# Hybrid decoder trunk on one core: the sums of squares behind the hand-overs move from VectorE to GpSimd

## The chip, the cores and the metric

The kernel runs on one core of one Trainium2 chip. The metric is device time in microseconds (us) of one execution, taken as the median over the runs of the kernel. TensorE, VectorE (DVE in the profile), ScalarE (ACT) and GpSimd (POOL) each work through a queue of instructions in order; the order of every queue is fixed when the kernel is built.

## What is computed

Two layers of a decoder trunk over 272 positions (16 meta tokens and 256 real ones) and 2048 channels, in float32. Cut to what matters here:

```python
def rms_norm(x, g):
    y = x * rsqrt(mean(x * x, axis=-1) + EPS)
    return y * g

def hybrid_layer(x, ...):
    h = rms_norm(x, norm_mix_pre)
    proj = h @ w_in                       # four groups of heads follow
    mix = concat([o_diff, o_sb, o_ssm, o_ret])
    x = x + rms_norm(mix @ w_out, norm_mix_post)
    hf = rms_norm(x, norm_ffn_pre)
    ffn = (silu(hf @ w_gate) * (hf @ w_up)) @ w_down
    return x + rms_norm(ffn, norm_ffn_post)
```

Each layer has four norms over 2048 channels. The two called "pre" stand behind a residual add and ahead of a large product.

## The kernel before

Activations lie with channels on the 128 partitions: `x` is 16 chunks (KC = 16) of 128 x 272. Weights stream from HBM in units of 8 tiles of 128 x 128 (`raw`, three buffers). Each unit is split into two parts: ScalarE copies the rounded high part (`hi`, line 682), VectorE subtracts it from the raw unit (`lo`, line 694), and TensorE makes three matmuls for each tile (`tile_mm`, line 711), high times high, high times low, low times high; in the second layer's feed-forward part two matmuls, the first of double width (`pair_mm`, line 733). Up to four units are held split (SPB = 4). The raw buffer of a unit is free for the next DMA when its `lo` is done (lines 696 to 698).

**The hand-overs.** When a product that ends in a residual add is finished, `norm` (line 1884) makes the post norm of chunk 0, and `post` (line 1956) goes through the other chunks in batches of one to three: VectorE scales `y`, adds it into `x`, ScalarE writes the high part of the next product's input `xhl` and VectorE its low part (`low`, line 1960). TensorE starts the next product at once, with the input not yet normalised: `first_chunk` (line 748) and `run_group` (line 773) go through the 16 chunks for 7 output tiles in 7 banks of PSUM. The pre norm's factor is a number for each position and is applied afterwards, when VectorE takes the products out of PSUM and multiplies by `rbc` (`evac_in`, line 1755; `evac_gu`, line 2020).

`prenorm` (line 1680) finds that factor beside the products. Behind the three hand-overs (layer 0 in its middle, layer 0 to layer 1, layer 1 in its middle) it calls `sumsq2` (line 1659): ScalarE squares two chunks at a time into one of two buffers (`squares`, line 1664), VectorE adds each square into `a2` (line 1675), seven times, and at the end adds the two halves of `a2` into `acc` (line 1678). TensorE then sums `acc` over the partitions in one matmul into `pn` (line 1685), and ScalarE and VectorE make `rbc` from it (`rsqrt_m2`, line 830). `prenorm` in the first layer's start has no `sq` and goes through `sumsq` (line 1642).

In the page the adds are `yf<-yf` (middle of a layer, where the squares lie in `yf`) and `sq<-sq` (between the layers). VectorE's instructions all carry line 338, those of ScalarE 378, matmuls 397: the helpers that record them.

**What sets the order.** While the kernel is built, a planner (`Sched`, line 461) advances threads against a model of the engines (`Clock`, line 238): each instruction has a modelled cost, each engine a modelled time, and a thread's next step is issued when its inputs are near ready in that model (`ok`, line 515). The matmul into `pn` goes into TensorE's queue where the model has `acc` ready. On the chip each queue is worked off in that order, whatever the real times are.

Of the kernel before, what the change touches and what calls it, by code (L numbers as in the profile page):

```python
# [16 lines left out]
ALU = mybir.AluOpType  # L17
# [220 lines left out]
class Clock:  # L238
# [1 line left out]

    LOG = None

    LAT = {"P": 0.2, "V": 0.14, "A": 0.145, "D": 0.0, "X": 0.0}

    def __init__(self):
        self.t = {"P": 0.0, "V": 0.0, "A": 0.0, "D": 0.0}
        self.acc = {}
        self.prev = {}
        self.slots = {}
        self.dead = set()  # L250
        self.step_end = 0.0
        self.win, self.cols, self.fast = 0, 0.0, False
# [19 lines left out]
    def ready(self, ap, eng, write=False):  # L272
        name, lo, hi = self.region(ap)
        r = 0.0
        for a in self.acc.get(name, ()):
            if a[0] < hi and lo < a[1]:
                r = max(r, a[2] + (self.same(eng) if a[3] == eng else self.LAT[a[3]]))
                if write:
                    r = max(r, a[4])
        return r  # L280
# [4 lines left out]
    def op(self, eng, cost, outs, ins, lat=0.0, cols=None):  # L285
# [28 lines left out]
        if eng != "D":  # L314
            self.step_end = max(self.step_end, en + self.LAT[eng])
        return en


def _free(ap):
    n = 1  # L320
    for d in ap.shape[1:]:
        n *= d
    return n


def _psum(ap):
    return "PSUM" in str(ap.space)


class Vec:  # L330
# [3 lines left out]
    def __getattr__(self, name):  # L334
        fn = getattr(self.eng, name)

        def f(*args, **kw):
            r = fn(*args, **kw)  # L338
            if args:
                kw = dict(kw, out=args[0])  # L340
            out = kw["out"]
            ins = [v for k, v in kw.items() if k in ("in_", "in0", "in1", "data0", "data1") and hasattr(v, "ap")]
            sc = [v for k, v in kw.items() if k in ("scalar", "scalar1", "scalar2") and hasattr(v, "ap")]
            n = max([_free(out)] + [_free(a) for a in ins])
            ps = any(_psum(a) for a in ins + [out])
            fast = name in ("tensor_scalar", "tensor_copy", "memset") and not ps
            cost = 0.068 + n / (1920.0 if fast else 960.0) + 0.061 * len(sc)
            if name == "reciprocal":
                cost = 0.07 + n * 0.0063
            self.clk.op("V", cost, [out], ins + sc)  # L350
            return r
        return f


class Act:
# [105 lines left out]
class Sched:  # L461
# [9 lines left out]
    def add(self, gen, prio, ready=0.0):  # L471
        th = Thread()
        th.gen, th.prio, th.done, th.end = gen, prio, False, ready
        th.ready = ready
        self.threads.append(th)
        self._advance(th)
        return th
# [86 lines left out]
def hybrid_trunk_kernel(ctx, tc, xT, wst, prm, ssm, b3, gpo, cst, msk, out, cfg=None, dbg=None):  # L564
    cfg = cfg or {}
    nc = tc.nc
    clk = Clock()
    V, A, PE = Vec(clk, nc.vector), Act(clk, nc.scalar), Ten(clk, nc.tensor)
    sched = Sched(clk, A, {"V": cfg.get("LV", 1.2), "A": cfg.get("LA", 1.0), "slack": cfg.get("slack", 0.15), "low": cfg.get("low", 0.4), "tab": cfg.get("tab", 4.0)})
    NU = wst.shape[0]  # L570
    RAWB = cfg.get("raw", 3)
    SPB = cfg.get("spl", 4)
# [46 lines left out]
    P = const.tile([128, DEPTH, NPC], F32, name="P")  # L619
# [931 lines left out]
    acc = rb_p.tile([128, T], F32, name="acc")  # L1551
# [107 lines left out]
    def sumsq2(src, n, sq, ready, prio):  # L1659

        qs = []
        a2 = sq(0)

        def squares():
            for k in range(0, KC, 2):
                yield ("A", lambda: ready(k + 1) if len(qs) < 2 else None)
                q = a2 if k == 0 else sq(1 + k // 2 % 2)
                A.activation(out=q, in_=src[:, k:k + 2], func=AF.Square)
                if k:
                    qs.append(q)  # L1670

        sched.add(squares(), prio)
        for k in range(2, KC, 2):
            yield ("V", lambda: clk.ready(qs[0], "V") if qs else None)
            V.tensor_tensor(out=a2, in0=a2, in1=qs[0], op=ALU.add)
            qs.pop(0)
        yield "V"
        V.tensor_tensor(out=acc[:, :n], in0=a2[:, 0], in1=a2[:, 1], op=ALU.add)

    def prenorm(src, n, pl, ready, alloc, psum, prio=0, sq=None):  # L1680

        yield from sumsq2(src, n, sq, ready, prio) if sq else sumsq(src, n, pl, ready, prio)
        yield ("P", alloc)
        ps = psum()
        PE.matmul(ps[:, :n], nones, acc[:, :n], start=True, stop=True)
        t0 = pl.tile([128, T], F32, tag="t", name="pn")[:, :n]
        yield from rsqrt_m2(ps[:, :n], rbc[:, :n], t0, -float(DM))
        alloc[0].rel(alloc[1], ps)
        yield "V"
        V.tensor_scalar(out=rbc[:, :n], in0=rbc[:, :n], scalar1=0.5 / DM, scalar2=None, op0=ALU.mult)  # L1690
        S["rbc"] = True
# [495 lines left out]
```

## Time and profile before

| | |
|---|---|
| median of 3 runs | 2417.64 us (2416.16 to 2419.79) |
| profiled execution, its own time | 2417.29 us |
| span of the profiled execution | 2415.5 us |
| TensorE busy | 2397.3 us, 99% |
| VectorE busy | 1666.3 us, 69% |
| ScalarE busy | 1318.1 us, 55% |
| GpSimd busy | 0.2 us, 4 instructions |

"Busy" counts the time from an instruction's start to its end; matmuls overlap, so a busy TensorE says only that something was under way. Where TensorE waits is read from the list of waits and from the number of matmuls in equal stretches. The granted clock of TensorE is shown for each stretch as a share of full speed: 1.00 is 2.4 GHz, 0.50 is 1.2 GHz.

### The profile page before, as it was taken

What the parts mean: (1) busy time and instruction counts of PE and PEld (TensorE: products, weight loads), DVE (VectorE), ACT (ScalarE), POOL (GpSimd) and SP (SyncE); (2) the same over time, 40 slices, a digit from 0 to 9 for tenths busy, and PEclk for the clock granted to TensorE, in tenths of its full rate; (3) what the DMA queues carried; (4) which work ended last, traced back from release to release, by engine and by line L of the source; (5) the groups of instructions that cost most, each with busy time, mean ns of one, the idle gap of its engine ahead of it and who ended that gap; (6) DMA issues with size and microseconds to landing.
All of it is one profiled execution on the core that took longest, in us unless ns stands there. A gap on an engine that the chain in (4) does not pass through costs nothing.

```text
span 2415.5 us, 42961 instructions
## 1 busy us (share of the span) xinstructions
PE 2397.3 (99%) x17211; PEld 2264.2 (94%) x17211; DVE 1666.3 (69%) x2768; ACT 1318.1 (55%) x2159; POOL 0.2 (0%) x4
## 2 busy tenths in 40 slices
PE   9999999999999999999999999999999999999998
PEld 9999999999999999999999999999888888888886
DVE  7999997885554455555568999978766544666654
ACT  6587766644433344444456777657894444444443
POOL 0000000000000000000000000000000000000000
PEclk9999999999999999999999999999999999999999
DMA  7544455555555555555545544455556555555564
GB/s 257 168 149 131 150 162 174 168 188 175 175 177 177 175 175 175 175 175 174 176 138 168 166 156 148 160 185 163 182 187 201 189 187 191 185 190 188 192 197 156
DMA packets 123096, 423.07 MB, mean 175 GB/s; under 512 B 15120, under 2 KB 18960, under 8 KB 122896
## 3 DMA queue, kind: packets, MB, share of 16 engines
q1 hardware_dynamic: 122896, 420.33, 53.7%
q8 instruction: 135, 2.21, 0.4%
q14 instruction: 65, 0.53, 0.1%
HBM read 414.83 MB, written 2.10 MB: 173 GB/s over the span
## 4 chain that ended last, share of the span: by engine, by line
PE 96%; DVE 2%; ACT 1%; DMA 0%; issue 0%; SPq 0%; DVEq 0%; ACTq 0%
PE mmps L397 92%; PE sd L397 3%; PE sd L409 1%; DVE lo L338 0%; PE sc L397 0%; DMA raw<-in_w_dram 0%; PE yp L397 0%; DVE x L338 0%; ACT hi L378 0%; DVE yf L338 0%; ACT tab L378 0%; DVE xhl L338 0%; DVE p L338 0%; DVE sq L338 0%; ACT sq L378 0%
## 5 line engine op out<-in xcount | busy, mean ns | idle before, releaser
L397 PE MATMUL mmps<-xhl,hi 128*128 128x272 f32 (+2 forms) x7047 | 1568.4, 310 | 0.0
L338 DVE TENSOR_TENSOR lo<-raw,hi 128x1024 fp32r<-128x1024 f32 (+1 forms) x772 | 939.6, 1219 | 583.3 <-ACT hi L378 582.3
L378 ACT ACTIVATE hi<-raw 128x1024 fp32r<-128x1024 f32 (+1 forms) x772 | 813.3, 1056 | 851.1 <-PE mmps L397 643.7
L397 PEld LDWEIGHTS mmps<-xhl,hi 128*128 128x128 f32 x7047 | 1155.6, 189 | 65.2 <-issue 3.0
L397 PE MATMUL mmps<-xhl,lo 128*128 128x272 f32 (+1 forms) x4224 | 1212.4, 287 | 2.1 <-DVE lo L338 2.1
L397 PEld LDWEIGHTS mmps<-xhl,lo 128*128 128x128 f32 x4224 | 797.1, 189 | 3.5 <-DVE lo L338 2.7
L397 PE MATMUL mmps<-hh,hi 128*128 128x272 f32 x704 | 202.7, 288 | 0.0
L397 PE MATMUL mmps<-hl,hi 128*128 128x272 f32 x704 | 202.6, 288 | 0.0
L397 PE MATMUL mmps<-hh,lo 128*128 128x272 f32 x704 | 202.2, 287 | 0.0
L397 PE MATMUL mmps<-ml,hi 128*128 128x272 f32 (+1 forms) x544 | 155.4, 286 | 0.0
L397 PE MATMUL mmps<-mh,hi 128*128 128x272 f32 (+1 forms) x544 | 154.9, 285 | 0.0
L397 PE MATMUL mmps<-mh,lo 128*128 128x272 f32 (+1 forms) x544 | 154.9, 285 | 0.0
L397 PE MATMUL mmps<-lo,hh 128*128 128x512 f32 x344 | 135.9, 395 | 0.0
L397 PE MATMUL mmps<-hi,hh 128*128 128x512 f32 x344 | 135.9, 395 | 0.0
L397 PE MATMUL mmps<-hi,hl 128*128 128x512 f32 x344 | 135.9, 395 | 0.0
L397 PEld LDWEIGHTS mmps<-hh,lo 128*128 128x128 f32 x704 | 132.5, 188 | 0.0
L397 PEld LDWEIGHTS mmps<-hh,hi 128*128 128x128 f32 x704 | 132.5, 188 | 0.0
L397 PEld LDWEIGHTS mmps<-hl,hi 128*128 128x128 f32 x704 | 132.3, 188 | 0.0
L397 PEld LDWEIGHTS mmps<-ml,hi 128*128 128x128 f32 x544 | 102.3, 188 | 0.9 <-issue 0.8
L397 PEld LDWEIGHTS mmps<-mh,hi 128*128 128x128 f32 x544 | 102.6, 189 | 0.5 <-issue 0.4
L397 PEld LDWEIGHTS mmps<-mh,lo 128*128 128x128 f32 x544 | 102.6, 189 | 0.0
L397 PEld LDWEIGHTS mmps<-hi,hl 128*128 128x128 f32 x344 | 64.6, 188 | 15.7
(324 smaller groups left out, 1862.8 us busy)
## 6 DMA issues: line engine op xcount, KB each, us to landing
raw<-in_w_dram SPq DMA_DIRECT2D x771, 512.0 KB, 3.5
b3r<-in_b_dram SPq DMA_DIRECT2D x16, 192.0 KB, 3.7
u3r<-uh SPq DMA_DIRECT2D x64, 34.0 KB, 2.1
out_dram<-xt SPq DMA_DIRECT2D x8, 256.0 KB, 2.3
x<-in_x_dram SPq DMA_DIRECT2D x7, 272.0 KB, 5.6
cs<-in_cst_dram SPq DMA_DIRECT2D x5, 256.0 KB, 6.1
u3r<-ul SPq DMA_DIRECT2D x32, 34.0 KB, 2.1
cc<-in_ssm_dram SPq DMA_DIRECT2D x2, 512.0 KB, 5.7
```

Of the source, the lines that this page charges most:

```text
L338: r = fn(*args, **kw)
L378: r = self.eng.activation(out=out, in_=in_, func=func, **kw)
L397: r = self.eng.matmul(out, lhsT, rhs, **kw)
L409: r = self.eng.transpose(out, in_, ident)
```

## The change

A wrapper for GpSimd's add is put beside the wrapper for VectorE, with a cost and a latency for the planner's model. In `sumsq2`, the seven adds and the last one that folds `a2` into `acc` are issued on GpSimd, behind all three hand-overs. The squares stay on ScalarE, the two buffers stay two, and the first norm of the kernel (`sumsq`) is not touched.

```diff
-    LAT = {"P": 0.2, "V": 0.14, "A": 0.145, "D": 0.0, "X": 0.0}
+    LAT = {"P": 0.2, "V": 0.14, "A": 0.145, "D": 0.0, "X": 0.0, "G": 0.3}
...
-        self.t = {"P": 0.0, "V": 0.0, "A": 0.0, "D": 0.0}
+        self.t = {"P": 0.0, "V": 0.0, "A": 0.0, "D": 0.0, "G": 0.0}
...
+class Gps(Vec):
+    def add(self, out, in0, in1):
+        self.eng.tensor_tensor(out=out, in0=in0, in1=in1, op=ALU.add)
+        self.clk.op("G", 0.2 + _free(out) * 0.0022, [out], [in0, in1])
...
+    G = Gps(clk, nc.gpsimd)
-    sched = Sched(clk, A, {"V": cfg.get("LV", 1.2), "A": cfg.get("LA", 1.0), "slack": cfg.get("slack", 0.15), "low": cfg.get("low", 0.4), "tab": cfg.get("tab", 4.0)})
+    sched = Sched(clk, A, {"V": cfg.get("LV", 1.2), "A": cfg.get("LA", 1.0), "G": 1.0, "slack": cfg.get("slack", 0.15), "low": cfg.get("low", 0.4), "tab": cfg.get("tab", 4.0)})
...
         for k in range(2, KC, 2):
-            yield ("V", lambda: clk.ready(qs[0], "V") if qs else None)
-            V.tensor_tensor(out=a2, in0=a2, in1=qs[0], op=ALU.add)
+            yield ("G", lambda: clk.ready(qs[0], "G") if qs else None)
+            G.add(a2, a2, qs[0])
             qs.pop(0)
-        yield "V"
-        V.tensor_tensor(out=acc[:, :n], in0=a2[:, 0], in1=a2[:, 1], op=ALU.add)
+        yield "G"
+        G.add(acc[:, :n], a2[:, 0], a2[:, 1])
```

## Rows read from the trace of the kernel before

**Rows 1.** The page, part 1: busy us, share of the span, instructions.
```profile
PE 2397.3 (99%) x17211; PEld 2264.2 (94%) x17211; DVE 1666.3 (69%) x2768; ACT 1318.1 (55%) x2159; POOL 0.2 (0%) x4
```

**Rows 2.** Chain that ended last, middles of the layers: start, us, what.
```profile
441.55 38.30 PE mmps L397 x307
479.85 0.46 PE pn L397 x2
...
1662.19 35.70 PE mmps L397 x222
1697.88 0.43 PE pn L397 x2
```

**Rows 3.** TensorE's waits, 1236 to 1300 us: total us, times, longest.
```profile
PE pn L397 <- DVE acc L338: 2.5, 1, 2.5
PE mmps L397 <- DVE lo L338: 1.9, 2, 1.6
```

**Rows 4.** Busy time between the layers by 2 us, and the sum over 1240 to 1300.
```profile
1276.00:1278.00 2.00, 2.00 (x10) 1.89 (x9) 2.00 (x3) 1.00 (x3) 0.00 (x0) 0.52 0.39 160
1278.00:1280.00 2.00, 2.00 (x13) 2.00 (x12) 1.90 (x4) 0.81 (x1) 0.00 (x0) 0.62 0.71 221
1280.00:1282.00 2.00, 2.00 (x18) 2.00 (x18) 1.51 (x2) 0.25 (x1) 0.00 (x0) 1.00 0.83 248
...
sum 60.00, PE 55.51 PEld 53.50 DVE 47.72 ACT 32.51 POOL 0.00; mean PE 1.85 PEld 1.78 DVE 1.59 ACT 1.08 POOL 0.00
```

**Rows 5.** Busy time, 15 us behind each hand-over: PE, PEld, DVE, ACT, POOL, clock, DMA.
```profile
445.00:460.00 15.00, 15.00 (x120) 14.89 (x119) 14.90 (x24) 10.60 (x17) 0.00 (x0) 1.00 0.31 107
1245.00:1260.00 15.00, 13.39 (x106) 13.17 (x106) 13.78 (x24) 8.75 (x16) 0.00 (x0) 1.00 0.16 55
1665.00:1680.00 15.00, 15.00 (x97) 13.29 (x95) 14.69 (x26) 10.91 (x19) 0.00 (x0) 1.00 0.34 106
```

**Rows 6.** Instructions on the tiles yf and sq: min/median/max ns, first and last start.
```profile
L338 DVE TENSOR_TENSOR yf<-yf x14: 680/702/725, 449.6 to 1694.4; 128x544 f32<-128x544 f32 x7, 128x512 f32<-128x512 f32 x7
L338 DVE TENSOR_TENSOR acc<-yf x2: 418/425/432, 477.8 to 1695.4; 128x272 f32<-128x272 f32 x1, 128x256 f32<-128x256 f32 x1
L338 DVE TENSOR_TENSOR sq<-sq x7: 715/725/726, 1249.6 to 1274.1; 128x544 f32<-128x544 f32 x7
```

**Rows 7.** VectorE in order of time, between the layers: start, us, what, idle before.
```profile
1249.56 0.72 DVE L338 TENSOR_TENSOR sq<-sq 128x544 f32<-128x544 f32 x1 [0.46 <-ACT sq L378]
...
1265.55 0.72 DVE L338 TENSOR_TENSOR sq<-sq 128x544 f32<-128x544 f32 x1
1266.20 1.22 DVE L338 TENSOR_TENSOR lo<-raw,hi 128x1024 fp32r<-128x1024 f32 x1
...
1275.13 0.43 DVE L338 TENSOR_TENSOR acc<-sq 128x272 f32<-128x272 f32 x1
```

**Rows 8.** VectorE, two prices: a two-input scan, and a one-input operation.
```profile
L338 DVE TENSOR_TENSOR_SCAN z<-rho,p 128x272 f32<-128x272 f32 x64 | 42.7, 708 | 0.4
...
1280.00 0.30 DVE L338 TENSOR_SCALAR rbc<-rbc 128x272 f32<-128x272 f32 x1
```

**Rows 9.** TensorE and VectorE in order of time, middles of the layers.
```profile
445.04 0.39 PE L397 MATMUL mmps<-xhl,hi 128*128 128x272 f32 x1
...
464.10 0.49 DVE L338 SCALAR_TENSOR_TENSOR xhl<-x,P,xhl 128x272 fp32r<-128x272 f32 x1
474.58 0.72 DVE L338 TENSOR_TENSOR yf<-yf 128x544 f32<-128x544 f32 x1 [0.79 <-ACT yf L378]
477.82 0.43 DVE L338 TENSOR_TENSOR acc<-yf 128x272 f32<-128x272 f32 x1
...
1695.38 0.42 DVE L338 TENSOR_TENSOR acc<-yf 128x256 f32<-128x256 f32 x1
```

**Rows 10.** ScalarE in order of time: last squares, middle of layer 0 and between layers.
```profile
474.87 0.64 ACT L378 ACTIVATE yf<-x 128x544 f32<-128x544 f32 x1
...
1272.59 0.64 ACT L378 ACTIVATE sq<-x 128x544 f32<-128x544 f32 x1
```

## The prediction

> **What bounds the kernel now.** I read the page's engine totals first. TensorE is busy for 99% of the span and GpSimd does 4 instructions in all [rows 1], so a change that only unloads VectorE can win time only where TensorE waits for VectorE. I looked for such places in the chain that ended last and in TensorE's waits around the three hand-overs. In the middle of layer 0 the chain is TensorE alone, 38.30 us of matmuls and then the matmul into pn, with no wait between; in the middle of layer 1 the same, 35.70 us [rows 2]. Only between the layers does TensorE wait: 2.5 us for acc and 1.9 us for lo, in two pieces [rows 3]. The stretches of 2 us show the rest of the loss there: from 1240 to 1300 us TensorE is busy 55.51 of 60 us, and behind the wait for acc its granted clock is at 0.52 and 0.62, with 10 and 13 matmuls where the next stretch has 18 [rows 4], that is (8 + 5) x 2/18 = 1.4 us. So 4.5 + 1.4 = 5.9 us is all that a faster VectorE could give back, 0.24% of the run.
>
> The other thing to see is how full VectorE is there: 14.90, 13.78 and 14.69 of 15 us behind the three hand-overs [rows 5]. In the middles of the layers it just keeps up. TensorE starts chunk 0 at 445.04 and makes 21 matmuls for each chunk, 120 of them in 15 us [rows 5], so it wants chunk 8 at 445.04 + 8 x 21 x 0.125 = 466.0; VectorE finishes that chunk's low part at 464.10 + 0.49 = 464.6 [rows 9], 1.4 us ahead. And acc is ready at 477.82 + 0.43 = 478.25 and 1695.80 [rows 9], while pn starts at 479.85 and 1697.88 [rows 2]: 1.6 and 2.1 us of room.
>
> **What is removed.** VectorE loses 21 adds of two chunks and 3 last adds of one: 14 yf<-yf, 7 sq<-sq, 2 acc<-yf [rows 6] and one acc<-sq [rows 7]. An add shows 0.72 us, but the next instruction starts 0.65 us after it [rows 7], and that is what VectorE gets back; the last add, half as long, gives some 0.35. One hand-over: 7 x 0.65 + 0.35 = 4.9 us.
>
> **What is added.** The same 24 adds on GpSimd, which has no work like it in the trace. Its price I bound from below by VectorE's own 0.72 us [rows 6] and from above by the slowest two-input row per element, the scan with 708 ns for 272 elements, 1.42 us for 544 [rows 8]. The planner's formula in the diff gives 0.2 + 544 x 0.0022 = 1.40 us, next to the upper row; I take 1.40, and 0.70 for the last add. Seven and one make 10.5 us in each hand-over, in a chain, because every add writes a2 again. The squares come over some 26 us, so the chain as such fits.
>
> The GPSIMD Engine Reference of the Trainium skill (section on performance versus the Vector engine) gives 4497 ns for an add of 2048 elements; an estimate from that page is 4497 x 544/2048 = 1.19 us, by which the sum below would be some 3 us smaller. No run here shows it.
>
> **What the adds do to VectorE** is the term that decides, and no row shows the two engines side by side. The lower end is nothing: both run freely. The upper end is that the adds and VectorE's two-input operations take turns. What rows say is this: an operation with one input in SBUF takes 0.30 us for 272 elements, one with two inputs 0.43 [rows 7, 8]. VectorE moves through a single operand faster than through two, so with two it already uses all the reading that this trace shows it can do. In these stretches nearly everything on VectorE has two inputs in SBUF (lo from raw and hi, y from y and r, x from x and y, the low part from x and xhl). I take the upper end: turns. Then an add costs VectorE 1.40 instead of giving back 0.65, a difference to before of 0.75 us, 0.35 for the last.
>
> The page "SBUF — State Buffer" of the Trainium skill (section "Who interferes with whom") says that a VectorE instruction with two SBUF inputs contends with a GpSimd instruction that reads SBUF, and that the one that comes second is blocked for the whole instruction. By that rule the upper end holds; by free running the sum would be that of the first rival. No run here shows it yet.
>
> **The sum, by place.**
> - Middle of layer 0: VectorE is 7 x 0.75 + 0.35 = 5.6 us later at acc; 0.79 us of idle time [rows 9] takes some of it: 4.8. GpSimd's answer to TensorE is a little slower than VectorE's (0.30 against 0.14 us in the diff): 5.0. The room at pn is 1.6: TensorE loses 3.4 us. Part of it would fall earlier, since chunk 8 has only 1.4 us of room, but each such stop moves pn as well, so this counts once. rbc comes as much later as acc; the 7 banks fill later too, by TensorE's own loss, so I add nothing there.
> - Middle of layer 1: the same 5.6 + 0.2 less 2.1 of room: 3.7 us.
> - Between the layers: 5 of the 7 adds start before VectorE's last lo ahead of the wait (first at 1249.56, fifth at 1265.55 [rows 7]); there VectorE itself is the limit, so 5 x 0.75 = 3.8 us goes to TensorE in full. The last square ends at 1272.59 + 0.64 = 1273.2 [rows 10]; add six is then half done, so add six's rest, add seven and the fold take 0.7 + 1.4 + 0.7 = 2.8, to 1276.0 and the hop, against 1275.6 before: 0.6. Turns behind a lo of 1.22 us at each of the three: some 0.6 each, 1.8. A longer stop keeps the clock at the lower level for longer; 1.4 us was lost so before, and I add 0.5. Together 6.7 us.
> - Nothing is moved past a DMA queue. A raw buffer is freed by lo, so weights come as much later as lo does; between the layers this is inside the 3.8 us, in the middles the weights' lead takes it.
>
> Sum: 3.4 + 3.7 + 6.7 = 13.8 us. On the profiled execution's own 2417.29 us (span 2415.5, 1.8 around it) that is 2431.1; the median of the runs lies 0.35 us higher, so 2431.4 for a median. Its own range: with adds at 1.19 to 1.42 us it moves by 3 to 4 us, and since the planner believes VectorE to be 4.9 us freer it will put pn earlier in TensorE's queue, up to 3 us in each hand-over, which I left at nothing: 2426 to 2441.
>
> **Rivals.**
> - *Free running* (not slower): the adds don't touch VectorE. For it: no row shows a contention. Between the layers VectorE is 5 x 0.65 = 3.2 us ahead; two adds ahead of the first wait for lo take 1.3 of its 1.6 us, the second wait goes as well (0.3), the wait for acc shrinks by the remaining 1.6 less the slower end of the chain (0.6), and half of the clock's 1.4 comes back: 1.6 + 1.0 + 0.7 = 3.3 us. The middles give nothing, TensorE doesn't wait there. 2417.64 - 3.3 = 2414.3, no change by what can be measured (0.2%, 4.8 us). A gain over 4.8 us needs nearly all of the 5.9. It decides if VectorE's lo and x instructions start as close together as before while an add runs.
> - *Slow adds alone*: VectorE undisturbed, an add twice the upper row, 2.8 us. In the middle of layer 0 the last two adds and the fold end 2.8 + 2.8 + 1.4 = 7.0 us after the second last square (some 474.6): 481.6, 1.8 late at pn; layer 1 alike, 2; between the layers some 1 net of VectorE's relief. Plus 5 us, 2422.5, at the edge of what can be measured.
> - *GpSimd never gets its turn* while VectorE works back to back: the squares' two buffers stay full, ScalarE stops behind the third square and takes the high parts of the input with it, and the adds run only in stops: 10.5 us in each hand-over, less 1.6 and 2.1 of room: plus 28 us, 2445. Against it: ScalarE would leave VectorE idle soon, and then turns come.
>
> **How the numbers follow.** Turns 0.55, free running 0.25, slow adds alone 0.12, no turn 0.08. Free running is faster by over 0.2% in two cases of five: 0.10, and 0.02 for a lucky new order elsewhere: 0.12. Within 0.2%: the rest of free running and half of the slow adds, and a few cases of mild turns: 0.27. Slower: 0.61. Cases of both signs don't hold most of the chance, but free running must be in the range: low 2412.5, high 2443; what is left out is a gain of nearly the whole ceiling and most of the last rival.
>
> **What would show it.** GpSimd has 28 instructions instead of 4. Right: starts on VectorE around an add lie up to 1.4 us apart where they were back to back, TensorE waits for acc on GpSimd at pn in all three places, and 1260 to 1290 has a longer stretch below full clock. Wrong: VectorE's busy stretches shorter by 4.9 us at each hand-over and no wait at pn in the middles of the layers.

## The result, and the profile after

The changed kernel takes 2430.12 us (2429.44 to 2431.37, four runs) against 2416.9 us before (2415.61 to 2419.79, four runs). The ratio is 1.0054, interval 1.0036 to 1.0071: slower by 13 us. 2431.4 us was forecast, 13.8 us over the time before, with turns between GpSimd and VectorE as the cause.

The page of the changed kernel, part 1, answers to [rows 1]:

```profile
PE 2399.1 (99%) x17209; PEld 2264.3 (93%) x17209; DVE 1675.8 (69%) x2744; ACT 1317.7 (54%) x2159; POOL 41.8 (2%) x28
```

GpSimd has the 24 adds, and VectorE has 24 instructions less. Yet VectorE is busy for longer, 1675.8 us instead of 1666.3: its other instructions have become slower. The adds took 15 to 16 us of the time before [rows 6, 7], so the others take some 25 us more, about 1 us for each of the 24 adds on GpSimd.

Where the time went is found with a mark that both traces have in the same place of the work: ScalarE's square of the last tile ahead of each hand-over. The first three lines are of the kernel before, the others of the changed one (ScalarE in order of time: start, us, what, idle before).

```profile
440.38 0.40 ACT L378 ACTIVATE sq<-mmps 128x272 f32<-128x272 f32 x1 [1.68 <-PE mmps L397]
...
1240.31 0.40 ACT L378 ACTIVATE sq<-mmps 128x272 f32<-128x272 f32 x1 [2.06 <-PE mmps L397]
...
1661.05 0.38 ACT L378 ACTIVATE sq<-mmps 128x256 f32<-128x256 f32 x1 [1.50 <-PE mmps L397]
```
```profile
440.68 0.40 ACT L384 ACTIVATE sq<-mmps 128x272 f32<-128x272 f32 x1 [1.68 <-PE mmps L403]
...
1244.02 0.40 ACT L384 ACTIVATE sq<-mmps 128x272 f32<-128x272 f32 x1 [2.06 <-PE mmps L403]
...
1668.84 0.38 ACT L384 ACTIVATE sq<-mmps 128x256 f32<-128x256 f32 x1 [1.50 <-PE mmps L403]
```

The distances from mark to mark tell what each hand-over costs, with all that follows it up to the next mark: the middle of layer 0 is 803.34 - 799.93 = 3.4 us longer, the one between the layers 424.82 - 420.74 = 4.1 us, and from the last mark to the end of the span (2427.4 and 2415.5) it is 758.56 - 754.45 = 4.1 us. Ahead of the first mark the two traces differ by 0.3 us. Such a distance is one execution's: between the layers it also moves by about 1 us in a kernel whose median does not change (spare_memsets below), in the middles of the layers by less than 0.2.

TensorE's longest waits in the three stretches (440 to 500, 1244 to 1300 and 1668 to 1725 us, in order of time: start, us, what, idle before) answer to [rows 2, 3]:

```profile
474.24 0.39 PE L403 MATMUL mmps<-xhl,lo 128*128 128x272 f32 x1 [1.12 <-DVE lo L338]
479.02 0.73 PE L403 MATMUL pn<-acc,nones 128*128 128x272 f32 x2 [1.73 <-POOL acc L357]
...
1259.43 0.39 PE L403 MATMUL mmps<-xhl,lo 128*128 128x272 f32 x1 [1.27 <-DVE lo L338]
1269.87 0.39 PE L403 MATMUL mmps<-xhl,lo 128*128 128x256 f32 x1 [1.22 <-DVE lo L338]
1275.19 0.39 PE L403 MATMUL mmps<-xhl,lo 128*128 128x272 f32 x1 [2.07 <-DVE lo L338]
1279.93 1.27 PE L403 MATMUL pn<-acc,nones 128*128 128x272 f32 x2 [3.84 <-POOL acc L357]
...
1706.96 0.70 PE L403 MATMUL pn<-acc,nones 128*128 128x256 f32 x2 [0.71 <-POOL acc L357]
...
1717.46 1.03 PE L403 MATMUL mmps<-nones 128*128 128x256 bf16 x8 [1.63 <-DVE ga L338]
```

In the middles of the layers TensorE did not wait before [rows 2]; now it waits for lo, for acc at pn and, in layer 1, for the first bank to be emptied (ga); two waits of 0.5 us there, for xhl and for lo, are left out above. Between the layers the waits for lo grow from 1.9 to 4.6 us and the one for acc from 2.5 to 3.8 us.

What happens on VectorE is seen best in the middle of layer 0. These are the VectorE instructions of the changed kernel, 445 to 480 us, that are longer than their kind, with the GpSimd adds beside them (order of time; a line with x2 or x3 has merged neighbours and gives the sum):

```profile
449.99 4.08 POOL L357 TENSOR_TENSOR yf<-yf 128x544 f32<-128x544 f32 x2 [449.54 <-ACT yf L384]
458.91 1.37 POOL L357 TENSOR_TENSOR yf<-yf 128x544 f32<-128x544 f32 x1 [4.84 <-ACT yf L384]
462.88 2.24 POOL L357 TENSOR_TENSOR yf<-yf 128x544 f32<-128x544 f32 x1 [2.60 <-ACT yf L384]
468.98 2.03 POOL L357 TENSOR_TENSOR yf<-yf 128x544 f32<-128x544 f32 x1 [3.86 <-ACT yf L384]
474.30 3.75 POOL L357 TENSOR_TENSOR yf<-yf 128x544 f32<-128x544 f32 x2 [3.29 <-ACT yf L384]
478.13 0.84 POOL L357 TENSOR_TENSOR acc<-yf 128x272 f32<-128x272 f32 x1
```
```profile
450.89 1.95 DVE L338 TENSOR_TENSOR lo<-raw,hi 128x1024 fp32r<-128x1024 f32 x1 [0.36 <-ACT hi L384]
452.76 1.89 DVE L338 TENSOR_TENSOR y<-y,r 128x544 f32<-128x544 f32 x1
...
458.94 2.05 DVE L338 SCALAR_TENSOR_TENSOR xhl<-x,P,xhl 128x272 fp32r<-128x272 f32 x2
...
463.82 2.16 DVE L338 TENSOR_TENSOR y<-y,r 128x816 f32<-128x816 f32 x1
...
469.70 2.43 DVE L338 SCALAR_TENSOR_TENSOR xhl<-x,P,xhl 128x272 fp32r<-128x272 f32 x3
...
475.25 4.02 DVE L338 SCALAR_TENSOR_TENSOR xhl<-x,P,xhl 128x272 fp32r<-128x272 f32 x3
```

Undisturbed these take 1.22, 0.72, 0.91, 1.00, 1.32 and 1.32 us in the kernel before. The surplus is 0.73 + 1.17 + 1.14 + 1.16 + 1.11 + 2.70 = 8.0 us, for eight GpSimd instructions: 1.0 us for each. Every add shows up as a delay of the one or two VectorE instructions next to it and of no others. An add that starts on its own takes 1.37 us; one that comes while a VectorE instruction runs shows 2.0 to 2.2, so its span seems to hold the waiting too.

Between the layers the clock is low for longer than in [rows 4] (2 us each: PE, PEld, DVE, ACT, POOL, granted clock, DMA):

```profile
1276.00:1278.00 2.00, 0.09 (x1) 0.00 (x0) 2.00 (x3) 1.42 (x3) 1.92 (x2) 0.58 0.84 279
1278.00:1280.00 2.00, 0.07 (x1) 0.07 (x1) 2.00 (x2) 1.06 (x1) 1.80 (x2) 0.50 0.73 244
1280.00:1282.00 2.00, 2.00 (x7) 1.76 (x8) 2.00 (x3) 0.73 (x2) 0.00 (x0) 0.50 0.01 2
1282.00:1284.00 2.00, 2.00 (x14) 2.00 (x14) 1.90 (x5) 0.19 (x1) 0.00 (x0) 0.72 0.90 293
```

After the wait for acc TensorE works at the lower level until some time past 1282 us and makes 7 and 14 matmuls where 18 go at full clock; before it was 10 and 13.

TensorE's queue has changed too. The matmul into pn now stands behind 240 matmuls on xhl in the middle of layer 0, 175 between the layers and 184 in the middle of layer 1; before, it stood behind 274, 203 and 190 (matmuls on the tile xhl from the start of the hand-over to pn, as counted in the traces).

### The profile page after: what moved, and what is told of

It is laid out like the page before. It is cut to its first block, busy times and chain, and to the rows that moved or that the text cites. A ratio compares the mean times of both kernels' runs of the same rounds, so it can differ in the third digit from the quotient of the medians.

```text
span 2427.4 us, 42976 instructions
## 1 busy us (share of the span) xinstructions
PE 2399.1 (99%) x17209; PEld 2264.3 (93%) x17209; DVE 1675.8 (69%) x2744; ACT 1317.7 (54%) x2159; POOL 41.8 (2%) x28
## 4 chain that ended last, share of the span: by engine, by line
PE 93%; DVE 4%; ACT 1%; issue 1%; DMA 0%; POOL 0%; SPq 0%; DVEq 0%; POOLq 0%; ACTq 0%
PE mmps L403 89%; PE sd L403 3%; DVE lo L338 1%; DVE y L338 1%; PE sd L415 1%; DVE xhl L338 1%; DVE x L338 1%; DMA raw<-in_w_dram 0%; PE sc L403 0%; PE yp L403 0%; ACT hi L384 0%; DVE yf L338 0%; ACT tab L384 0%; ACT xhl L384 0%; DVE p L338 0%
```

## The experiments

Three explanations were open: GpSimd's adds block VectorE (the theory); the planner's new order costs the time (rival 1); the adds are only slow, so acc comes late (rival 2).

**Is it the engine or the order? (plan_on_vector)** Only the engine of the adds is set back; TensorE's queue is the changed kernel's.

```diff
-    G = Gps(clk, nc.gpsimd)
+    G = Gps(clk, nc.vector)
```

> The changed kernel with one word undone: the 24 adds are issued on VectorE again, at the places where the planner that believes them to be on GpSimd puts them, so TensorE's order is that of the changed kernel. Theory (the adds on GpSimd block VectorE's two-input operations): without GpSimd at work nothing is blocked, 2414 to 2421 us. Rival 1 (the new order is to blame: matmul into pn too early, other order of lo): the loss stays, 2427 to 2432 us. Rival 2 (GpSimd is merely slow, so acc comes late, VectorE is not disturbed): near 2417 us as well, so the next run has to tell it from the theory.

Measured: 2423.48 us, ratio 1.0025 (1.0015 to 1.0034) to the kernel before. Neither value came: 5.8 us of the loss stay with nothing on GpSimd, and 6.6 go. By the marks, 1.2, 3.3 and 1.0 us of the loss in the three hand-overs come with this order. TensorE's waits in it, the three hand-overs one after the other:

```profile
PE pn L403 <- DVE acc L357: 1.0, 1, 1.0
...
PE pn L403 <- DVE acc L357: 4.2, 1, 4.2
PE mmps L403 <- DVE lo L338: 3.5, 3, 1.7
...
PE mmps L403 <- DVE ga L338: 0.6, 1, 0.6
PE pn L403 <- DVE acc L357: 0.4, 1, 0.4
```

The planner believes VectorE to be free of the adds and GpSimd to be done with them earlier than is so, and puts pn where acc isn't ready. Undone in this sequence, the two causes share the loss about evenly in total, but not in each place: the engine is worth 2.2, 0.8 and 3.1 us by the marks, the order 1.2, 3.3 and 1.0. (The planner doesn't count these adds on VectorE, so the 5.8 us hold that mistake too.)

**Does GpSimd cost time when nobody waits for it? (spare_adds)** The kernel before with its own order; behind each add a GpSimd add on the same buffer whose result nobody reads. The squares get eight buffers instead of two, so that none of them waits for GpSimd.

```diff
-                q = a2 if k == 0 else sq(1 + k // 2 % 2)
+                q = a2 if k == 0 else sq(k // 2)
...
             V.tensor_tensor(out=a2, in0=a2, in1=qs[0], op=ALU.add)
-            qs.pop(0)
+            q = qs.pop(0)
+            nc.gpsimd.tensor_tensor(out=q, in0=q, in1=q, op=ALU.add)
...
```

> The kernel before, its own adds on VectorE and its own order, and behind each of the 21 adds of two chunks one GpSimd add of the same size on the square's buffer that nothing waits for (eight buffers instead of two, so that no square waits for GpSimd). Theory: each spare add holds VectorE up for up to 1.37 us, 9.6 us in a hand-over, part of it where VectorE has room: 2427 to 2442 us, and VectorE operations of 1.9 us and more beside the adds. Rival 2 (only a late acc costs time): 2417 us, since nobody waits for the spare adds. Rival 1 (order): 2417 us.

Measured: 2431.89 us, ratio 1.0059 (1.0044 to 1.0074). The loss is there, 14.2 us, with the old order and with no one waiting for GpSimd: 4.0, 6.0 and 4.0 us in the three hand-overs. Rival 2 falls as the whole cause. VectorE's busy time rises by 17.8 us over the kernel before, to 1684.1. Its instructions stretch as above: first one that takes 0.50 us alone, then one that takes 0.72, and the GpSimd add beside the first.

```profile
460.07 1.33 DVE L338 SCALAR_TENSOR_TENSOR xhl<-x,P,xhl 128x272 fp32r<-128x272 f32 x1
...
462.37 1.61 DVE L338 TENSOR_TENSOR x<-x,y 128x544 f32<-128x544 f32 x1
...
456.27 4.83 POOL L1677 TENSOR_TENSOR yf<-yf 128x544 f32<-128x544 f32 x1 [3.98 <-DVE yf L338]
```

This add's span is 4.83 us, and of the VectorE instructions that start in it before 461 us only the one at 460.07 is held up. So an add can also stand back for several VectorE instructions in a row: turns are not strictly one by one.

**Is it any work on GpSimd? (spare_memsets)** The same triggers, the same eight buffers, but three memsets in place of each add, which write and don't read.

```diff
+            for _ in range(3):
+                nc.gpsimd.memset(q, 0.0)
...
```

> As spare_adds, but three GpSimd memsets of the same buffer in place of each add: GpSimd writes and reads nothing. Theory in its narrow form (the two engines take turns at reading SBUF): VectorE is not disturbed, 2415 to 2420 us. In a wide form (any GpSimd work beside VectorE, or its semaphores, costs VectorE time): as spare_adds, 2425 us and more.

Measured: 2417.7 us, ratio 1.000 (0.9991 to 1.001). GpSimd's groups in it (count, busy us, mean ns):

```profile
L1678 POOL MEMSET sq<- 128x544 f32 x21 | 11.7, 555 | 786.6 <-DVE sq L338 785.8
L1678 POOL MEMSET yf<- 128x544 f32 x21 | 11.6, 553 | 466.5 <-DVE yf L338 465.7
L1678 POOL MEMSET yf<- 128x512 f32 x21 | 11.0, 527 | 410.5 <-DVE yf L338 409.7
```

34 us of GpSimd beside a full VectorE, 1.8 us at a time, cost nothing, and VectorE's busy time stays at 1666.7 us. It is GpSimd's reading that costs, not its work as such, its writing or its semaphores. This is what the Trainium skill's page "SBUF — State Buffer" (section "Who interferes with whom") says of a VectorE instruction with two SBUF inputs: it contends with a GpSimd instruction that reads, not with one that only writes. The runs agree: 14.2 us against none.

**Which VectorE instructions are blocked? (long_row_of_gpsimd)** The kernel before; from the middle of layer 0 on GpSimd works through three long rows on a tile of its own. A copy from rbc ahead of them, not shown, sets the start.

```diff
...
+            for _ in range(60):
+                nc.gpsimd.tensor_tensor(out=g[:, 0], in0=g[:, 0], in1=g[:, 1], op=ALU.add)
+            for _ in range(100):
+                nc.gpsimd.tensor_copy(out=g[:, 0], in_=g[:, 1])
+            for _ in range(200):
+                nc.gpsimd.memset(g[:, 0], 0.0)
```

> The kernel before, and from the middle of layer 0 on, while the gate and up products run, GpSimd works through 60 adds, then 100 copies, then 200 memsets of 128 x 544 on a tile of its own that nothing waits for. Theory: beside the adds VectorE's operations with two inputs in SBUF (ga from ga and rbc, hl from gb and hh, lo from raw and hi) stretch by some 0.5 us and more on average, those with one input in PSUM (ga from mmps and rbc, gb from mmps and ga) keep their 0.43 us but for what precedes them; beside the memsets none stretches. Beside the copies, which read one input: as beside the adds if reading at all is what excludes, but shorter. Rival (VectorE undisturbed): all forms keep their times throughout.

Measured: 2480.55 us in one run, 63 us over the kernel before. VectorE's groups by form (count, busy us, mean ns), first beside the adds (485 to 581 us), then beside the copies (582 to 684), then beside the memsets (686 to 806):

```profile
L338 DVE TENSOR_TENSOR lo<-raw,hi 128x1024 fp32r<-128x1024 f32 x11 | 23.5, 2140 | 0.0
L338 DVE TENSOR_TENSOR ga<-ga,rbc 128x272 f32<-128x272 f32 x6 | 5.4, 900 | 0.0
L338 DVE SCALAR_TENSOR_TENSOR lea<-lea,lef 128x2 f32<-128x2 f32 x7 | 4.3, 609 | 0.0
L338 DVE TENSOR_TENSOR gb<-mmps,ga 128x272 f32<-128x272 f32 x6 | 2.6, 432 | 0.0
...
L338 DVE TENSOR_TENSOR lo<-raw,hi 128x1024 fp32r<-128x1024 f32 x34 | 47.8, 1406 | 17.3 <-ACT hi L378 17.3
L338 DVE TENSOR_TENSOR ga<-ga,rbc 128x272 f32<-128x272 f32 x8 | 6.5, 814 | 0.0
L338 DVE TENSOR_TENSOR gb<-mmps,ga 128x272 f32<-128x272 f32 x8 | 3.5, 436 | 3.0 <-PE mmps L397 3.0
...
L338 DVE TENSOR_TENSOR lo<-raw,hi 128x1024 fp32r<-128x1024 f32 x41 | 50.5, 1232 | 47.8 <-ACT hi L378 47.8
L338 DVE TENSOR_TENSOR ga<-ga,rbc 128x272 f32<-128x272 f32 x8 | 3.5, 433 | 0.0
```

With both inputs in SBUF, lo goes from 1232 ns beside memsets to 2140 beside adds, and ga<-ga,rbc from 433 to 900. With one input in PSUM, gb<-mmps,ga keeps its 432 to 436 ns beside adds and copies. The length of the blocked instruction doesn't matter: lea<-lea,lef has two columns, takes 156 ns alone and 609 on average here, and this one waits for nearly a whole add:

```profile
528.15 1.32 DVE L338 SCALAR_TENSOR_TENSOR lea<-lea,lef 128x2 f32<-128x2 f32 x1
```

So the price is for each GpSimd instruction that meets VectorE, not for each element that VectorE moves. From 485 to 581 us TensorE makes 334 matmuls, in the kernel before 767 in the same stretch, at a granted clock of 0.75 against 1.00.

**What would a planner do that knew? (planner_told)** The changed kernel; the model holds VectorE while GpSimd adds.

```diff
+        self.clk.t["G"] = self.clk.t["V"] = max(self.clk.t["G"], self.clk.t["V"])
         self.clk.op("G", 0.2 + _free(out) * 0.0022, [out], [in0, in1])
+        self.clk.t["V"] = self.clk.t["G"]
```

> The changed kernel, with the planner's model holding VectorE for as long as GpSimd adds. Theory: VectorE loses the same 0.7 us more per add than before, but the matmul into pn and the low parts are put where they can be met: 2420 to 2427 us. If most of the loss is the matmul into pn standing too early in TensorE's queue: 2417 to 2420 us. If the order has no part in it: 2428 to 2431 us.

Measured: 2424.65 us, ratio 1.0032 (1.0019 to 1.0045). No wait at pn is left in any hand-over. By the marks the middles of the layers lose more than in the changed kernel (5.0 and 4.7 us), now because pn (behind 325 and 216 matmuls on xhl instead of 274 and 190) and with it the factor rbc come too late for the banks: TensorE waits 2.0 and 1.3 us for ga, and 0.5 and 1.8 us for xhl. The list of waits doesn't show all of it. Where the model has TensorE idle at the start of a group of output tiles, the planner puts in filler matmuls whose result is not used (`keep_warm`, line 1623 of the kernel before; mmps<-nones in bf16 in the profile). These are TensorE's fillers behind the two waits for ga:

```profile
490.64 2.23 PE L405 MATMUL mmps<-nones 128*128 128x256 bf16 x19 [1.98 <-DVE ga L338]
...
1710.66 2.23 PE L405 MATMUL mmps<-nones 128*128 128x256 bf16 x19 [1.33 <-DVE ga L338]
```

The kernel before has none in the first place and 10 in the second (1.26 us), so they make another 2.2 and 1.0 us. Between the layers this kernel is 3.1 us shorter than the one before the change.

**The hand-over between the layers by itself.** First, the kernel before with the adds on VectorE and with their old price, but with a lower rank for their thread in this hand-over (adds_last_between_layers).

```diff
-        sched.add(prenorm(x, T, t2, lambda k: clk.ready(x[:, k], "A") if S["nsum"] > k else None, CY, cyt, 0, lambda i: sqt[:, i]), cfg.get("sq", 0))
+        sched.add(prenorm(x, T, t2, lambda k: clk.ready(x[:, k], "A") if S["nsum"] > k else None, CY, cyt, 1, lambda i: sqt[:, i]), cfg.get("sq", 1))
```

> The kernel before, adds on VectorE, but between the layers the thread of the sums of squares has a lower rank than the input of the next product, so the adds come behind what TensorE waits for. If the 5.9 us lost there are VectorE's load in the wrong order: 2412 to 2415 us. If the adds are not what holds lo up: 2417 us. If rbc comes too late for the banks of PSUM: over 2418 us.

Measured: 2415.6 us, ratio 0.9991 (0.9982 to 1.0): 1.9 us by the medians, less than hoped, with an interval that reaches 1. By the marks the 1.9 us are all between the layers. The wait for acc falls from 2.5 to 0.4 us, those for lo rise from 1.9 to 3.2.

Then three kernels in which the middles of the layers issue their adds on VectorE as before, and only those between the layers go through `G`; the first with the change's own price (gpsimd_between_layers_only), the second with the planner told as above (told_between_layers_gpsimd), the third told and with `G` on VectorE (told_between_layers_vector). The last two lines of the diff are of the third alone; the lines that tell the planner are those above.

```diff
+            e = "G" if gp else "V"
+            yield (e, lambda: clk.ready(qs[0], e) if qs else None)
+            if gp:
+                G.add(a2, a2, qs[0])
+            else:
+                V.tensor_tensor(out=a2, in0=a2, in1=qs[0], op=ALU.add)
...
-    G = Gps(clk, nc.gpsimd)
+    G = Gps(clk, nc.vector)
```

> The change made between the layers alone; in the middles of the layers the adds stay on VectorE. If the hand-overs pay each for itself, as the distances between them in the changed kernel's trace say (4.1 us between the layers, 3.4 and 4.1 in the middles): 2420 to 2423 us. If the loss in one hand-over is passed on to the next: outside that.

Measured: 2423.04 us, ratio 1.0021 (1.0012 to 1.0031), 5.4 us, at the upper edge of what was expected. By the marks this hand-over costs 6.1 us here and 4.1 in the full change. The order differs: pn stands behind 154 matmuls on xhl here and behind 175 there. The order that the planner finds depends on what came before, so hand-overs don't quite pay each for itself.

> As gpsimd_between_layers_only, with the planner holding VectorE while GpSimd adds. In planner_told this hand-over was 3.1 us shorter than before the change, the two others 5.0 and 4.7 us longer. If hand-overs pay each for itself: 2413 to 2416 us, faster than before the change though GpSimd still blocks VectorE, by an order alone.

Measured: 2415.42 us, ratio 0.9992 (0.9984 to 1.0001), so not told apart from the kernel before.

> The same order as told_between_layers_gpsimd with these adds issued on VectorE. If the order (matmul into pn later) is the gain and GpSimd's blocking still costs some: 2410 to 2414 us, the fastest of all. If unloading VectorE was the gain: 2415 to 2419 us, slower than with GpSimd.

Measured: 2412.43 us, ratio 0.998 (0.9971 to 0.9989), the fastest of all, faster than either kernel. The two share one order, instruction for instruction in this hand-over; GpSimd in place of VectorE costs 3.0 us in it. TensorE's only wait between 1236 and 1310 us, and its busy time in the 60 us in which the kernel before had 425 matmuls:

```profile
PE mmps L405 <- DVE lo L338: 0.3, 1, 0.3
```
```profile
1240.00:1300.00 60.00, 59.67 (x475) 57.56 (x474) 53.42 (x94) 37.99 (x64) 0.00 (x0) 1.00 0.45 144
```

The gain that the change looked for was there, close to the 5.9 us of the prediction's ceiling, but it lay in the order: the planner had to believe the adds dear, and they had to stay on VectorE. In the new order pn stands behind 283 matmuls on xhl instead of 203, and acc is made some 3 us later; other VectorE instructions have moved as well, and which of the moves brings the gain isn't shown. A later pn isn't all of it: in adds_last_between_layers pn stands behind 188.

## Why the prediction was right

- **The sum** came within 1.3 us of the measured time, and part of that is luck: the price of the turns was too high and the price of the new order was left at nothing, and the two nearly cancel (below). The signs named in advance came: 28 instructions on GpSimd, waits for acc on GpSimd at pn in all three places, and a longer stretch below full clock.
- **The ceiling** of 5.9 us was not put to the test: no run unloads VectorE without blocking it. The largest gain found, 5.2 us, came from an order that unloads nothing, and lies below it.
- **Turns.** The term that decides was taken at its right end: GpSimd's adds and VectorE's two-input operations get in each other's way when both read (spare_adds against spare_memsets). The argument from the rows, that two inputs use all the reading VectorE can do, fits the rows with an input in PSUM, which are not held up, but it is too narrow: instructions that read one tensor, in SBUF, were held up as well (last section).
- **The price of an add** was taken at 1.40 us, 1.37 was measured where it starts at once. What it takes from VectorE is less: 8.0 us for the eight instructions in the middle of layer 0, where 7 x 1.40 + 0.70 = 10.5 were charged. The term was 2.5 us too big there, some 0.3 us an add; why an add of 1.37 us holds VectorE for less than its length isn't shown. An add of 1.19 us, the prediction's other estimate, was not seen: the shortest of this size takes 1.23 us (spare_adds). Nor does "some 3 us smaller" follow from the sum: 0.21 us less in each add takes 7.5 x 0.21 = 1.6 us from each middle and 7 x 0.21 = 1.5 from the stretch between the layers, 4.6 in all.
- **Middle of layer 0:** 3.4 us forecast, 3.4 measured, but made up otherwise. VectorE was to be 5 us late at acc. In fact acc is done at 478.97, 0.4 us later than before when the marks are laid on each other. Against the 8.0 us that the blocking took stand the 4.9 that the adds gave back, and much of the rest fell on lo: VectorE has done 8 of them by the end of its low parts where it had done 10. The loss arose from pn, which the planner put 34 matmuls earlier in TensorE's queue (1.7 us of waiting), and from a late lo (1.1 us). The prediction had named the earlier pn as a bound (up to 3 us) and left it at nothing in the sum, so that the 3.4 us agree is luck.
- **Middle of layer 1:** 3.7 forecast, 4.1 measured. The wait at pn was smaller (0.7), and 1.6 us is a wait for the first bank to be emptied. "I add nothing there" was wrong by that much. The factor rbc is ready at 1711.0 instead of 1701.0, which is 2.2 us later when the marks are laid on each other, but the bank is emptied only from 1714.9 on. In between ScalarE waits for two units of weights:

```profile
1711.88 1.06 ACT L384 ACTIVATE hi<-raw 128x1024 fp32r<-128x1024 f32 x1 [2.31 <-DMA raw<-in_w_dram]
1713.96 1.06 ACT L384 ACTIVATE hi<-raw 128x1024 fp32r<-128x1024 f32 x1 [1.02 <-DMA raw<-in_w_dram]
```

ScalarE's copies out of the banks (ga<-mmps, from 1714.93) stand behind these two in its queue. On VectorE the lo of the second unit (1715.06 to 1716.28) stands ahead of its part of the emptying. The two units came 3.6 and 4.5 us after the lo that free their raw buffers (1708.3 and 1709.5), and these lo were late. So "in the middles the weights' lead takes it" failed here.
- **Between the layers:** 6.7 forecast, 4.1 measured in the full change and 6.1 with the change made there alone. The two orders differ, and TensorE waits 4.6 us for lo in the one and 6.1 in the other, so the 4.1 came of an order that happened to be kinder; how much of the gap to 6.7 is the over-priced add isn't shown.
- The rivals: free running is excluded by spare_adds, slow adds alone by the same run, and no-turn by the changed kernel's trace, where no add spans more than 2.3 us. In spare_adds one add spans 4.83 us, so an add can lose several turns. What the prediction lacked was a separate term for the order: plan_on_vector shows that 5.8 of the 13 us come with it, and the sum reached the total by charging all of it to the blocking.

## What to carry to other kernels

An engine that looks idle isn't free if its reads hold up the busy one: moving an add of two SBUF inputs from VectorE to GpSimd gave VectorE 0.65 us back and took 1.0 from it. Where an order is planned by a model, a change in a model's costs moves the order as well; separate the two with a kernel that keeps the new order on the old engine, since here they were worth about the same in total. And look at what is queued before looking for another engine: the 5 us lay in another order of the same instructions.

## What the runs showed of the hardware that was not expected

- A VectorE instruction on two columns waits for a whole GpSimd add: 1.32 us in place of 0.16.
- It isn't only two-input VectorE work: beside the adds, two TENSOR_SCALAR of 128 x 16, which by the profile read one tensor, took 1284 ns on average, where such a one takes 0.17 us in the kernel before. Others of that kind in the stretch were held up in the same way.

```profile
L338 DVE TENSOR_SCALAR e1k<-e1k 128x16 f32<-128x16 f32 x2 | 2.6, 1284 | 0.0
```

- GpSimd's copies of 128 x 544, which read one input, take 977 ns on average (640 at the least) and block too, for less: lo takes 1406 ns beside them, 1232 beside memsets. Its memsets of the same size take 553 ns and block nothing.
